# Attention scores with the low part of the keys as two 64-row products, and one score phase per head pair in the first layer

## The chip, the core and the metric

The kernel runs on one core of a Trainium2 chip. The metric is device microseconds (us) of one execution of the whole program; smaller is better. The time before is the median of three runs.

## The reference, cut to what matters

The program is a two-layer decoder trunk on 256 tokens of width 2048. Each layer normalises, projects to queries, keys, values and a gate, attends, multiplies by the gate, projects back and adds. The first layer ("fox") has 32 heads of 64 with a bias from cumulated forget gates; the second ("swa") has 32 query heads on 4 key heads, a window of 128 keys and a sink. The scores, which are the part that changes:

```python
# first layer, for each block of 128 queries
s = einsum('bqhd,bkhd->bhqk', qi, kf) * scale
s = s + ci[..., None] - c[:, :, None, :]
s = where(mask, s, NEG_INF); p = softmax(s)
# second layer
s = einsum('bqhgd,bnkhd->bnhgqk', qb, kw) * scale
s = where(mask, s, NEG_INF)
m = maximum(max(s), sink); e = exp(s - m)
p = e / (sum(e) + exp(sink - m))
```

## The kernel before, in words

**Two-part numbers.** Operands of the large products are split into a high part of reduced precision (type fp32r) and the low rest. Every weight tile `w`, 128 rows deep, comes from HBM as `wraw`; ScalarE copies the high part (line 224), VectorE subtracts to get the low part (line 225), and TensorE makes products of 512 columns (high by both parts) and of 256 columns (low by high) into PSUM tiles called `acc`. All matmuls are issued by one helper, line 83, so the profile shows them under that line and tells them apart by tile.

**Order of the work.** TensorE runs in program order. The projections stream without end; after every second matmul of a weight piece a step counter advances (`tick`), and work on attention is hung on it: `after(steps, fn)` runs `fn` that many steps later, with priority over the stream in the scheduler. The tables `FOX_DUE`, `FOX_LAST`, `FOX_ODD`, `FOX_FIRST`, `FOX_NEXT` (first layer, by group) and `SWA_DUE`, `SWA_LAST` (second) hold these step counts. A group is four heads: two pairs `j = 0, 1` of two heads `hh = 0, 1`. There are eight groups to a layer, so 16 pairs to a layer.

**Scores of a pair.** A head is 64 deep, half of the array's 128 rows. `stack_q` puts a head's high queries on one half of the rows and its low queries on the other half; the keys stand as `kk[hh]` with part 0 (high) and part 1 (low), each copied to both halves. One product on 128 rows thus gives (high + low) queries by one part of the keys. `product` takes both parts of the keys side by side, so its output has high and low keys in different columns, which VectorE adds.

In the first layer (`Pair`) a pair's scores come in two phases. `s` handles the second block of queries (128 queries, 256 keys): two products of 512 columns, a VectorE add of the low columns and the bias `bc` into the score tile `st` (line 432), and for each head a fused add of the high columns with a running maximum (line 413). `s_first` follows `second` steps later with the first block (128 queries, 128 keys): two products of 256 columns, an add (line 444), two fused adds. Then come the softmax, a 32x32 transpose on VectorE, and a trip through HBM by DMA to turn the probabilities (`pts`). In the second layer (`JointPair`) `s` handles both blocks in one phase: two products of 256 columns for the first block, and for the second block four products of 256 columns, high and low keys of each head added in PSUM.

**Buffers.** The scores of all pairs use one PSUM buffer of two banks (tag `S`, one bank a head); queries (`q2`) and keys (`kk`) of the first layer have one buffer each. The bias of a pair is fetched by a DMA on SP's queue and masked by GpSimd (line 127); `early` issues that, `bias` steps ahead of `s`.

**Narrow products.** The products of probabilities and values (`psy`, `psy_s`) use part of the array: 128 rows by 64 columns in the first layer, 32 by 64 in the second, each on its own part. The first layer also transposes a 32-row tile once (`pt_c`). The profile writes such a shape as rows*columns, 128*64 for instance; whole products show 128*128.

Of the kernel before, what the change touches and what calls it, by code (L numbers as in the profile page):

```python
# [10 lines left out]
F32 = mybir.dt.float32  # L11
# [5 lines left out]
P = 128  # L17
S = 256
# [3 lines left out]
HD = 64  # L22
# [11 lines left out]
FORGOT = 22  # L34

SINK = 8
BIAS = 14
SCALE_DUE = 8


FOX_DUE = ((22, 12, 20), (50, 13, 30), 150)
FOX_LAST = ((24, 12, 20), (48, 13, 30), 134)
FOX_ODD = ((27, 13, 25), (56, 13, 35), 118)
FOX_FIRST = ((57, 16, 32), (81, 12, 40), 185)
FOX_NEXT = ((32, 15, 25), (64, 14, 40), 120)
SWA_DUE = ((36, 65), (53, 81), 91)
SWA_LAST = ((36, 63), (51, 78), 86)

SECOND = 10
LAST_HALF = 8  # L50
HALVES = 2
QBUFS = 1
# [9 lines left out]
def trunk(  # L62
# [16 lines left out]
    nc = tc.nc  # L79


    def mm(*args, **kw):
        tc.keep_in_program_order(nc.tensor.matmul(*args, **kw))  # L83
# [9 lines left out]
    work = ctx.enter_context(tc.tile_pool(name="work", bufs=2))  # L93
    dram = ctx.enter_context(tc.tile_pool(name="dram", bufs=1, space=bass.MemoryType.DRAM))
    ps_acc = ctx.enter_context(tc.tile_pool(name="ps_acc", bufs=2, space=bass.MemoryType.PSUM))
    ps_s = ctx.enter_context(tc.tile_pool(name="ps_s", bufs=1, space=bass.MemoryType.PSUM))
# [12 lines left out]
    def after(steps, fn):  # L109
        due.setdefault(clock[0] + max(steps, 1), []).append(fn)  # L110
# [54 lines left out]
    class Unit:  # L165


        def __init__(self, pieces, kind, consume, n=256, acts=None, halves=True, stages=(), acc=None, apart=None):

            self.kind, self.consume, self.n, self.halves = kind, consume, n, halves
            self.stages, self.acc = stages, acc or (ps_acc, "acc")

            self.apart = apart
            self.acts = xs if acts is None else acts
            self.parts, kt = [], 0
            for src, sizes in pieces:
                off = 0
                for s in sizes:  # L180
                    self.parts.append((src, off, sum(sizes), kt, s))
                    off += s
                    kt += s
            assert kt == KT
            self.ps = [None, None]
# [28 lines left out]
    def load(unit, p):  # L214
        src, off, _, _, s = unit.parts[p]
        n = unit.n
        ask(unit, p, nc.sync)
        raw = unit.raw[:, off : off + s, :]
        w = wpool.tile([P, 2048], F32R, tag="w", name="w")
        w = w[:, 0 : 2 * s * n].rearrange("p (k h n) -> p k h n", h=2, n=n)  # L220
        high, low = w[:, :, 0, :], w[:, :, 1, :]
        if isinstance(src, tuple):
            high, low = (a.rearrange("p k (g n) -> p k g n", g=2) for a in (high, low))
        state["split"] = nc.scalar.copy(high, raw)  # L224
        state["lows"] = [*state.get("lows", [])[-1:], nc.vector.tensor_tensor(  # L225
            out=low, in0=raw, in1=high.bitcast(F32), op=ALU.subtract
        )]
        loaded[unit, p] = w
# [10 lines left out]
    def block(unit, p, c, wide_first=None):  # L239
# [19 lines left out]

        first, last = kt0 == 0, kt0 + s == KT  # L260
        ops = [operands(i) for i in range(s)]
        def done():
            if p < len(unit.parts) - 1:
# [91 lines left out]
    BLK = ((slice(0, P), 0), (slice(P, 3 * P), 1))  # L355
# [28 lines left out]
    TOP, BOTTOM = slice(0, HD), slice(HD, P)  # L384
# [9 lines left out]
    class Pair:  # L394
# [10 lines left out]
        def product(self, out, hh, qb, keys):  # L405

            q2, kk = self.operands()
            mm(out, q2[:, hh, qb * P : (qb + 1) * P], kk[hh][:, :, 0:keys], start=True, stop=True)

        def reduce(self, high, hh, rng, qb, low=None):  # L410

            st = self.st[:, hh, rng]
            nc.vector.tensor_tensor_reduce(  # L413
                out=st, in0=high, in1=st if low is None else low, scale=self.scale, scalar=self.start(hh),
                op0=ALU.add, op1=self.extreme, accum_out=self.mx[:, qb, hh : hh + 1],
            )
# [7 lines left out]
        def s(self):  # L424

            self.st = work.tile([P, 2, 3 * P], F32, tag="st", name="st")
            self.mx = work.tile([P, 2, 2], F32, tag="mx", name="mx")
            rng, qb = BLK[1]
            ps = ps_s.tile([P, 2, 512], F32, tag="S", name="ps_s")
            for hh in range(2):  # L430
                self.product(ps[:, hh], hh, qb, S)
            nc.vector.tensor_add(self.st[:, :, rng], ps[:, :, S:], self.bias[:, :, rng])
            for hh in range(2):
                self.reduce(ps[:, hh, 0:S], hh, rng, qb)
            after(self.second, self.s_first)

        def s_first(self):

            rng, qb = BLK[0]
            ps = ps_s.tile([P, 2, 512], F32, tag="S", name="ps_s")[:, 0, :]  # L440
            ps = ps.rearrange("p (h a k) -> p h a k", h=2, k=P)
            for hh in range(2):
                self.product(ps[:, hh], hh, qb, P)
            nc.vector.tensor_add(self.st[:, :, rng], ps[:, :, 1, :], self.bias[:, :, rng])
            for hh in range(2):
                self.reduce(ps[:, hh, 0, :], hh, rng, qb)
            self.soft(self.st, self.mx)
            self.turn()

        def turn(self):  # L450

            staged = fox.tile([P, NB, 6, B], F32, tag="staged", name="staged", bufs=1)
            nc.vector.transpose(
                staged.rearrange("p b t i -> p t b i"),
                self.st.rearrange("p h (t b i) -> p (h t) b i", b=NB, i=B),
            )
            turned_d = dram.tile([NB, P, 6 * B], F32, tag="turned_d", name="turned_d", bufs=2)
            nc.gpsimd.dma_start(
                out=turned_d.rearrange("b p x -> p b x"), in_=staged.rearrange("p b t i -> p b (t i)")
            )  # L460
            pts = self.group.new_pts(self.j)[:, self.j]
            for b in range(NB):
                nc.gpsimd.dma_start(  # L463
                    out=pts[b * B : (b + 1) * B], in_=turned_d[b].rearrange("(a j) x -> j a x", j=B)
                )

        def later(self, group, s, second=SECOND, bias=BIAS):
            self.group, self.second = group, second
            after(s - bias, self.early)
            after(s, self.s)  # L470

    class JointPair(Pair):
# [5 lines left out]

            return self.sinks[:, 1, hh : hh + 1]

        def s(self):
            self.st = work.tile([P, 2, 3 * P], F32, tag="st", name="st")
            self.mx = work.tile([P, 2, 2], F32, tag="mx", name="mx")
            ps = ps_s.tile([P, 2, 512], F32, tag="S", name="ps_s2")
            first = ps[:, :, S:].rearrange("p h (a k) -> p h a k", k=P)
            q2, kk = self.operands()
            for hh in range(2):
                self.product(first[:, hh], hh, 0, P)
            for hh in range(2):
                for part in range(2):  # L490
                    mm(
                        ps[:, hh, 0:S], q2[:, hh, P : 2 * P], kk[hh][:, part, :],
                        start=part == 0, stop=part == 1,
                    )
            (rng0, _), (rng1, _) = BLK
            nc.vector.tensor_add(self.st[:, :, rng0], first[:, :, 1, :], self.bias[:, :, rng0])
            for hh in range(2):
                self.reduce(first[:, hh, 0, :], hh, rng0, 0)
            for hh in range(2):
                self.reduce(ps[:, hh, 0:S], hh, rng1, 1, self.bias[:, hh, rng1])  # L500
            self.soft(self.st, self.mx)

        def later(self, group, s, t):
            after(s, self.s)
# [58 lines left out]
    ones_row, z, a = (once[0:H, i * S : (i + 1) * S] for i in range(3))  # L563
# [33 lines left out]
    class FoxGroup(Group):  # L597
# [14 lines left out]
        def k(self, ps):  # L612
# [12 lines left out]

            due = (FOX_FIRST, FOX_NEXT, FOX_DUE, FOX_ODD)[min(self.g, 2 + self.g % 2)] if self.g < 7 else FOX_LAST

# [70 lines left out]
    for g, G in enumerate(groups):  # L698
        if g == 0:
            half, gt, st = (work, "half", 2 * S, HALVES), (work, "gt", 2 * S, 3), (work, "st", 6 * P, 2)  # L700
# [377 lines left out]
    start = [(u, p) for p in range(4) for u in (v0, q0, k0)]  # L1078
# [153 lines left out]
```

## Time and profile before

| | |
|---|---|
| median of the runs | 803.98 us (803.02 to 804.32, three runs) |
| profiled execution, its own time | 802.76 us |
| its span, first to last instruction | 801.0 us |
| TensorE (PE) busy | 790.0 us, 99% of the span |
| VectorE (DVE) busy | 646.9 us, 81% |
| ScalarE (ACT) busy | 516.2 us, 64% |
| GpSimd (POOL) busy | 104.8 us, 13% |
| granted TensorE clock | 0.998 of full speed |

A row of the timeline gives the start in us, the length in us, the engine, the line, the operation, output and input tiles, shape, count, and idle time before it. PE is the matmul stream, PEld the weight loads that run beside it. Because matmuls are pipelined and a listed length covers the whole pipeline, lengths of neighbours overlap: the pace is read from one start to the next.

### The profile page before, as it was taken

The numbers are of one execution on the slowest core, as the hardware profiler recorded it, in microseconds if no ns is written. First come the engines' busy times: TensorE is split into PE (matmuls) and PEld (weight loads), VectorE is DVE, ScalarE is ACT, GpSimd is POOL, SyncE is SP. The second block draws the span as 40 slices with busy tenths as digits, with TensorE's granted clock in tenths as the row PEclk, the third lists the DMA queues.
The fourth block names the chain that finished last, engine by engine and source line by source line (L and its number), as shares of the span: only waits on it lengthen the run. The fifth ranks groups of instructions, "written<-read, shape, count | busy, mean of one in ns | idle before, by whom it ended". The sixth has DMA issues, their size and how long they took to land.

```text
span 801.0 us, 13775 instructions
## 1 busy us (share of the span) xinstructions
PE 790.0 (99%) x4994; PEld 695.3 (87%) x4994; DVE 646.9 (81%) x1150; ACT 516.2 (64%) x950; POOL 104.8 (13%) x166
## 2 busy tenths in 40 slices
PE   8999999999999999999999999999999999999995
PEld 7988888888888888888888888888888888888885
DVE  6988987888788877889739868668998999976654
ACT  7776656665657566567446656477788886875651
POOL 1001331021301112021203200200000000001210
PEclk9999999999999999999999999999999999999999
DMA  8757887596766968677756665855545554456632
GB/s 289 258 193 258 242 279 248 174 280 221 243 204 193 286 228 247 187 219 228 222 174 206 220 193 169 222 156 190 183 152 187 165 184 157 161 190 186 204 112 105
DMA packets 54052, 164.44 MB, mean 205 GB/s; under 512 B 7024, under 2 KB 10256, under 8 KB 53984
## 3 DMA queue, kind: packets, MB, share of 16 engines
q1 hardware_dynamic: 47376, 148.13, 57.6%
q0 software_dynamic: 5456, 13.97, 6.1%
q10 hardware_dynamic: 1152, 1.47, 0.5%
q8 instruction: 39, 0.64, 0.3%
q14 instruction: 29, 0.24, 0.1%
HBM read 154.84 MB, written 8.70 MB: 204 GB/s over the span
## 4 chain that ended last, share of the span: by engine, by line
PE 94%; DVE 2%; DMA 2%; ACT 1%; issue 0%; SPq 0%; DVEq 0%; ACTq 0%
PE acc L83 88%; PE ps_s L83 3%; PE psy L83 2%; DMA wraw<-in_fox_in_dram 1%; DMA wraw<-in_vf_dram 1%; DVE w L225 1%; PE psy_s L83 0%; ACT st L361 0%; ACT w L224 0%; DVE scaled L866 0%; DVE kk L623 0%; SPq L211 0%; ACT q L390 0%; DVE st L413 0%; DVE st L372 0%
## 5 line engine op out<-in xcount | busy, mean ns | idle before, releaser
L83 PE MATMUL acc<-xs,w 128*128 128x256 f32 (+1 forms) x2624 | 468.2, 337 | 0.0
L83 PEld LDWEIGHTS acc<-xs,w 128*128 128x128 f32 x2624 | 404.3, 190 | 52.9 <-issue 0.7
L225 DVE TENSOR_TENSOR w<-wraw,w 128x1024 fp32r<-128x1024 f32 (+4 forms) x280 | 323.0, 1170 | 85.4 <-ACT w L224 84.3
L224 ACT CAST w<-wraw 128x1024 fp32r<-128x1024 f32 (+4 forms) x280 | 274.7, 1000 | 168.8 <-PE acc L83 113.3
L83 PE MATMUL acc<-ys,w 128*128 128x256 f32 (+1 forms) x960 | 168.3, 337 | 0.0
L83 PEld LDWEIGHTS acc<-ys,w 128*128 128x128 f32 x960 | 147.7, 190 | 19.4 <-issue 0.5
L83 PE MATMUL acc<-w,xs 128*128 128x512 f32 (+2 forms) x512 | 107.6, 361 | 1.0 <-ACT w L224 1.0
L83 PEld LDWEIGHTS acc<-w,xs 128*128 128x128 f32 x512 | 87.1, 189 | 15.8 <-ACT w L224 1.7
L361 ACT ACTIVATE st<-st,mx 128x256 f32<-128x256 f32 (+1 forms) x128 | 56.6, 444 | 16.6 <-DVE mx L680 9.2
L319 ACT COPY half<-acc 128x512 f32<-128x512 f32 x56 | 32.6, 583 | 28.8 <-PE acc L83 28.1
L463 POOL DMA_DIRECT2D pts<-turned_d x64 | 35.0, 553 | 75.0 <-DMA turned_d<-staged 51.0
L127 POOL TENSOR_SCALAR_AFFINE_SELECT bc<-bc 128x256 f32<-128x256 f32 x32 | 20.0, 647 | 169.9 <-DMA bc<-negc_d 109.5
L771 POOL TENSOR_TENSOR acc<-acc,sq 128x256 f32<-128x256 f32 x28 | 26.6, 950 | 80.9 <-ACT sq L765 79.7
L769 POOL COPY acc<-sq 128x256 f32<-128x256 f32 x2 | 1.5, 754 | 243.1 <-ACT sq L765 243.1
L83 PE MATMUL ps_s<-kk,q 128*128 128x256 f32 (+1 forms) x160 | 30.6, 305 | 0.8 <-DVE kk L624 0.8
L83 PEld LDWEIGHTS ps_s<-kk,q 128*128 128x128 f32 x160 | 25.0, 190 | 3.9 <-ACT w L224 1.0
L361 ACT ACTIVATION_READ_ACCUMULATOR st<-st,mx 128x1 f32 x128 | 24.0, 188 | 0.0
L380 ACT ACTIVATE st<-st,rl 128x128 f32<-128x128 f32 x64 | 23.9, 446 | 0.1
L159 DVE SCALAR_TENSOR_TENSOR xs<-xT,g_sb,xs 128x256 fp32r<-128x256 f32 x32 | 20.7, 680 | 3.4 <-ACT xs L158 3.4
L413 DVE CUSTOM_DVE_ANT_0 st<-ps_s,st 128x256 f32<-128x256 f32 (+1 forms) x64 | 20.2, 350 | 0.5
L158 ACT ACTIVATE xs<-xT,g_sb 128x256 fp32r<-128x256 f32 x32 | 15.4, 500 | 7.0 <-DVE xT L740 6.3
L509 DVE STREAM_TRANSPOSE turned<-st 128x768 f32<-128x768 f32 x16 | 15.6, 975 | 4.2 <-ACT st L380 4.0
(142 smaller groups left out, 563.2 us busy)
## 6 DMA issues: line engine op xcount, KB each, us to landing
wraw<-in_fox_in_dram SPq DMA_DIRECT2D x96, 512.0 KB, 5.1
wraw<-in_swa_in_dram SPq DMA_DIRECT2D x72, 512.0 KB, 4.4
wraw<-in_swa_out_dram SPq DMA_DIRECT2D x32, 512.0 KB, 4.9
wraw<-in_fox_out_dram SPq DMA_DIRECT2D x29, 512.0 KB, 4.4
wraw<-in_fox_in_dram SPq DMA_DIRECT2D x54, 256.0 KB, 4.7
bc<-negc_d SPq DMA_DIRECT2D x16, 384.0 KB, 5.7
turned_d<-staged POOLq DMA_DIRECT2D x16, 384.0 KB, 5.0
pts<-turned_d POOLq DMA_DIRECT2D x64, 96.0 KB, 5.4
```

The lines of the kernel that those rows point to most:

```text
L83: tc.keep_in_program_order(nc.tensor.matmul(*args, **kw))
L127: return nc.gpsimd.affine_select(out=ap, in_=ap, compare_op=ALU.is_ge, fill=NEG, base=base, pattern=pattern, channel_multiplier=mult,)
L159: nc.vector.scalar_tensor_tensor(out=xs[:, kt, 1, :], in0=xT[:, kt, :], scalar=g, in1=xs[:, kt, 0, :].bitcast(F32), op0=ALU.mult, op1=ALU. ...
L224: state["split"] = nc.scalar.copy(high, raw)
L225: state["lows"] = [*state.get("lows", [])[-1:], nc.vector.tensor_tensor(out=low, in0=raw, in1=high.bitcast(F32), op=ALU.subtract)]
L319: nc.scalar.copy(s, ps[:, :, S : 2 * S])
L361: nc.scalar.activation(st[:, hh, rng], st[:, hh, rng], AF.Exp, scale=sign, bias=nm[:, qb, hh : hh + 1], accum_out=l[:, qb, hh : hh + 1],)
L380: nc.scalar.mul(st[:, hh, rng], st[:, hh, rng], rl[:, qb, hh : hh + 1])
L413: nc.vector.tensor_tensor_reduce(out=st, in0=high, in1=st if low is None else low, scale=self.scale, scalar=self.start(hh), op0=ALU.add, o ...
L463: nc.gpsimd.dma_start(out=pts[b * B : (b + 1) * B], in_=turned_d[b].rearrange("(a j) x -> j a x", j=B))
L509: nc.vector.transpose(turned.rearrange("p h k -> p (h k)"), self.st.rearrange("p h k -> p (h k)"))
L771: nc.gpsimd.tensor_add(sums[0], sums[0], s)
```

## The change

The low queries by low keys are no longer computed for the second block of queries. Each head's high queries (64 rows) are multiplied with its low keys by a product of 64 rows, `cross`; the one of head 0 stands on rows 0 to 63 of the array, the one of head 1 on rows 64 to 127, and they add into two different PSUM banks on top of the products with the high keys. Both layers now use one `s`: two products of 256 columns for the first block, two of 256 columns for the second block by high keys, and the two `cross` products. `s_first` is gone, and so is VectorE's 512-column add of the first layer; the bias of the second block enters through the fused add. The tables shift: a first-layer pair has its one phase 8 steps later than its first phase was, which is 4 to 8 steps before its second phase was.

```diff
-FOX_DUE = ((22, 12, 20), (50, 13, 30), 150)
-FOX_LAST = ((24, 12, 20), (48, 13, 30), 134)
-FOX_ODD = ((27, 13, 25), (56, 13, 35), 118)
-FOX_FIRST = ((57, 16, 32), (81, 12, 40), 185)
-FOX_NEXT = ((32, 15, 25), (64, 14, 40), 120)
+FOX_DUE = ((30, 20), (58, 30), 150)
+FOX_LAST = ((32, 20), (56, 30), 134)
+FOX_ODD = ((35, 25), (64, 35), 118)
+FOX_FIRST = ((65, 24), (89, 40), 185)
+FOX_NEXT = ((40, 25), (72, 40), 120)
...
+        def cross(self, out, hh, qb):
+            q2, kk = self.operands()
+            rows = (TOP, BOTTOM)[hh]
+            mm(
+                out, q2[rows, hh, qb * P : (qb + 1) * P], kk[hh][rows, 1, :], start=False, stop=True,
+                tile_position=(hh * HD, 0),
+            )
...
         def s(self):
             self.st = work.tile([P, 2, 3 * P], F32, tag="st", name="st")
             self.mx = work.tile([P, 2, 2], F32, tag="mx", name="mx")
-            rng, qb = BLK[1]
             ps = ps_s.tile([P, 2, 512], F32, tag="S", name="ps_s")
+            first = ps[:, :, S:].rearrange("p h (a k) -> p h a k", k=P)
+            q2, kk = self.operands()
             for hh in range(2):
-                self.product(ps[:, hh], hh, qb, S)
-            nc.vector.tensor_add(self.st[:, :, rng], ps[:, :, S:], self.bias[:, :, rng])
+                self.product(first[:, hh], hh, 0, P)
             for hh in range(2):
-                self.reduce(ps[:, hh, 0:S], hh, rng, qb)
-            after(self.second, self.s_first)
-
-        def s_first(self):
-            rng, qb = BLK[0]
-            ps = ps_s.tile([P, 2, 512], F32, tag="S", name="ps_s")[:, 0, :]
-            ps = ps.rearrange("p (h a k) -> p h a k", h=2, k=P)
+                mm(ps[:, hh, 0:S], q2[:, hh, P : 2 * P], kk[hh][:, 0, :], start=True, stop=False)
             for hh in range(2):
-                self.product(ps[:, hh], hh, qb, P)
-            nc.vector.tensor_add(self.st[:, :, rng], ps[:, :, 1, :], self.bias[:, :, rng])
+                self.cross(ps[:, hh, 0:S], hh, 1)
+            (rng0, _), (rng1, _) = BLK
+            nc.vector.tensor_add(self.st[:, :, rng0], first[:, :, 1, :], self.bias[:, :, rng0])
             for hh in range(2):
-                self.reduce(ps[:, hh, 0, :], hh, rng, qb)
+                self.reduce(first[:, hh, 0, :], hh, rng0, 0)
+            for hh in range(2):
+                self.reduce(ps[:, hh, 0:S], hh, rng1, 1, self.bias[:, hh, rng1])
             self.soft(self.st, self.mx)
             self.turn()
```

In `JointPair` the second layer's own `s` goes (it had the same shape, with four 128-row products for the second block), and `turn` does nothing there.

Three places show what moves. First TensorE's program order in the first layer's group 2 (`ps_s` are the scores, `q_1420` its stacked queries), before and then after:

```order
L83 MATMUL acc<-xs,w 128x256 x28
L83 MATMUL ps_s<-kk,q_1420 128x512 x2
L83 MATMUL acc<-xs,w 128x256 x4
L83 MATMUL acc<-xs,w 128x512 x20
L83 MATMUL ps_s<-kk,q_1420 128x256 x2
L83 MATMUL acc<-xs,w 128x512 x12
L83 MATMUL acc<-xs,w 128x256 x20
L83 MATMUL ps_s<-kk,q_1420 128x512 x2
L83 MATMUL acc<-xs,w 128x256 x12
L83 MATMUL acc<-xs,w 128x512 x14
L83 MATMUL ps_s<-kk,q_1420 128x256 x2
```

```order
L81 MATMUL acc<-xs,w 128x256 x32
L81 MATMUL acc<-xs,w 128x512 x12
L81 MATMUL ps_s<-kk,q_1420 128x256 x6
L81 MATMUL acc<-xs,w 128x512 x20
L81 MATMUL acc<-xs,w 128x256 x32
L81 MATMUL acc<-xs,w 128x512 x4
L81 MATMUL ps_s<-kk,q_1420 128x256 x6
```

Each pair's 2 + 2 products, with a stretch of the stream between them, became one run of six; the last two of the six are the 64-row ones.

Second, TensorE's order in the first layer's last group, 7 (stacked queries `q_3655`), where its first scores stand, before and then after:

```order
L83 MATMUL acc<-xs,w 128x512 x32
L83 MATMUL acc<-xs,w 128x256 x32
L83 MATMUL ps_s<-kk,q_3655 128x512 x2
L83 MATMUL acc<-xs,w 128x512 x16
L83 MATMUL acc<-w,xs 128x512 x8
```

```order
L81 MATMUL acc<-xs,w 128x512 x32
L81 MATMUL acc<-xs,w 128x256 x32
L81 MATMUL acc<-xs,w 128x512 x16
L81 MATMUL ps_s<-kk,q_3655 128x256 x6
L81 MATMUL acc<-w,xs 128x512 x16
```

Sixteen products of 512 columns now stand ahead of this group's first scores.

Third, VectorE's order for group 2's first pair, from the last low part ahead of the scores on, before and then after (`ISA` is the fused add with its maximum, and the row `mx` behind it the write of that maximum):

```order
L225 TENSOR_TENSOR w<-wraw,w 128x4x256 x2
L432 TENSOR_TENSOR st<-ps_s,bc 128x2x256
L413 ISA st,mx<-ps_s,st 128x256
L413 ISA mx 128x1
L413 ISA st,mx<-ps_s,st 128x256
L413 ISA mx 128x1
L225 TENSOR_TENSOR w<-wraw,w 128x4x256
L348 TENSOR_TENSOR gt<-acc,half 128x512
L444 TENSOR_TENSOR st<-ps_s,bc 128x2x128
L349 TENSOR_TENSOR gt<-gt,r_n_492 128x512
L413 ISA st,mx<-ps_s,st 128x128
```

```order
L223 TENSOR_TENSOR w<-wraw,w 128x4x256 x3
L445 TENSOR_TENSOR st<-ps_s,bc 128x2x128
L420 ISA st,mx<-ps_s,st 128x128
L420 ISA mx 128x1
L420 ISA st,mx<-ps_s,st 128x128
L420 ISA mx 128x1
L420 ISA st,mx<-ps_s,bc 128x256
L420 ISA mx 128x1
L420 ISA st,mx<-ps_s,bc 128x256
L420 ISA mx 128x1
L346 TENSOR_TENSOR gt<-acc,half 128x512
```

The 512-element add (128x2x256) is gone, and the reading of the scores is one block on VectorE instead of two with a low part between them.

More of the change, by code (lines that the diff above doesn't have):

```diff
@@ L36 @@
 SINK = 8
-BIAS = 14
 SCALE_DUE = 8
-FOX_DUE = ((22, 12, 20), (50, 13, 30), 150)
-FOX_LAST = ((24, 12, 20), (48, 13, 30), 134)
-FOX_ODD = ((27, 13, 25), (56, 13, 35), 118)
-FOX_FIRST = ((57, 16, 32), (81, 12, 40), 185)
-FOX_NEXT = ((32, 15, 25), (64, 14, 40), 120)
+FOX_DUE = ((30, 20), (58, 30), 150)
[3 more added lines that the diff above has]
+FOX_NEXT = ((40, 25), (72, 40), 120)
 SWA_DUE = ((36, 65), (53, 81), 91)
 SWA_LAST = ((36, 63), (51, 78), 86)
-SECOND = 10
 LAST_HALF = 8
@@ L465, in turn, with later @@
                 )
-        def later(self, group, s, second=SECOND, bias=BIAS):
-            self.group, self.second = group, second
+        def later(self, group, s, bias):
+            self.group = group
             after(s - bias, self.early)
@@ L479, in start, with turn @@
             return self.sinks[:, 1, hh : hh + 1]
[L481 to L501, printed above, removed]
+        def turn(self):
+            pass
         def later(self, group, s, t):
```

## Prediction

> **What bounds the kernel.** First the page's head, its busy times and the chain of work that ended last, then the list of who TensorE waited for:
>
> ```profile
> span 801.0 us, 13775 instructions
> PE 790.0 (99%) x4994; PEld 695.3 (87%) x4994; DVE 646.9 (81%) x1150; ACT 516.2 (64%) x950; POOL 104.8 (13%) x166
> PE 94%; DVE 2%; DMA 2%; ACT 1%; issue 0%; SPq 0%; DVEq 0%; ACTq 0%
> ...
> PE rows L83 <- DVE tail L852: 2.1, 1, 2.1
> PE warm L83 <- DVE ones L120: 1.1, 1, 1.1
> PE acc L83 <- ACT w L224: 1.0, 2, 0.6
> PE ps_s L83 <- DVE kk L624: 0.8, 1, 0.8
> ```
>
> TensorE is busy for 99% of the span, 94% of the chain is its own work, and of its waits those at the start (`warm`, `acc`) and the end (`rows`) lie outside what is changed. So each nanosecond that the matmul stream gains or loses between them is one of the total, and the only wait that the change touches is the last row. The other engines matter only if they begin to make TensorE wait.
>
> **What the scores cost on TensorE now.** The timeline, cut to PE, around a first-layer pair's two phases, then around a second-layer pair:
>
> ```profile
> 377.82 0.63 PE L83 MATMUL ps_s<-kk,q 128*128 128x512 f32 x2
> 378.29 1.58 PE L83 MATMUL acc<-w,xs 128*128 128x256 f32 x12
> ...
> 385.44 0.40 PE L83 MATMUL ps_s<-kk,q 128*128 128x256 f32 x2
> 385.68 1.55 PE L83 MATMUL acc<-w,xs 128*128 128x512 f32 x6
> ...
> 703.59 0.88 PE L83 MATMUL ps_s<-kk,q 128*128 128x256 f32 x6
> 704.31 2.92 PE L83 MATMUL acc<-ys,w 128*128 128x256 f32 x13
> ```
>
> From start to start: two products of 512 columns take 378.29 - 377.82 = 0.47 us, 0.235 each; two of 256 take 0.24; a first-layer pair 0.71. Six of 256 in the second layer take 0.72, 0.12 each. Weight loads don't show in this pace: each runs beside the product ahead of it.
>
> **The change on TensorE.** A pair becomes four whole products of 256 columns (0.48) and two of 64 rows. If the two run side by side they need one slot, 0.12, for both: 0.60 in all. That is the gain, 0.11 for a first-layer pair and 0.12 for a second-layer one. But a 64-row product doesn't use the array as the stream around it does, and the trace of before has places where TensorE goes from whole products to narrow ones and back. The nearest by shape is `pt_c`, 32 rows by 128 columns; the timeline of PE there, then of PEld:
>
> ```profile
> 51.66 0.40 PE L83 MATMUL acc<-xs,w 128*128 128x512 f32 x1
> 51.98 0.24 PE L86 MATMUL pt_c<-ident,c 32*128 32x32 f32 x1
> ...
> 52.22 0.39 PE L83 MATMUL acc<-xs,w 128*128 128x256 f32 x1
> ...
> 52.45 0.40 PE L83 MATMUL acc<-xs,w 128*128 128x256 f32 x2
> ...
> 51.43 0.19 PEld L83 LDWEIGHTS acc<-xs,w 128*128 128x128 f32 x1
> 51.98 0.20 PEld L86 LDWEIGHTS pt_c<-ident,c 32*128 32x128 f32 x2 [0.36 <-issue]
> ```
>
> From the last whole product of 512 columns (51.66) to the second whole product behind the visit (52.45) are 0.79 us. At the stream's pace this holds 0.235 + 0.12 and two products of 32 columns, some 0.03 each by the pace of `pt_r` below (an estimate): 0.41. So the visit costs 0.38 beside its own work. The PEld row shows why: the narrow weight load does not run beside the product ahead, it starts 0.36 us after the last load ended. The same on the way back: 52.22 to 52.45 is 0.23 for a product of 256 columns that otherwise takes 0.12, since its weights were loaded in the open. The second view is a visit of `psy`, 128 rows by 64 columns, first its way in, then its way out:
>
> ```profile
> 379.35 0.52 PE L83 MATMUL acc<-w,xs 128*128 128x256 f32 x3
> 379.79 0.44 PE L83 MATMUL psy<-pts,vg 128*64 128x256 f32 x2
> ...
> 380.06 0.39 PE L83 MATMUL psy<-pts,vg 128*64 128x256 f32 x2
> ...
> 382.39 0.27 PE L83 MATMUL psy<-pts,vg 128*64 128x128 f32 x1
> 382.60 0.39 PE L83 MATMUL acc<-w,xs 128*128 128x256 f32 x1
> ...
> 382.82 0.40 PE L83 MATMUL acc<-w,xs 128*128 128x256 f32 x2
> ...
> 492.44 0.60 PE L86 MATMUL pt_r<-ident,xT 128*128 128x128 f32 x4
> ...
> 492.77 0.27 PE L86 MATMUL pt_r<-ident,xT 128*128 128x128 f32 x1
> ```
>
> Way in: three whole products from 379.35 would end their slots at 379.71, the narrow one starts at 379.79, 0.08 late; its first step takes 0.27, while 256 columns of full precision take 0.22 by `pt_r` (three starts of 128 columns in 492.77 - 492.44 = 0.33, 0.11 each), so 0.05 late. Way out: 0.21 where 128 columns take 0.11, 0.10 late; then 0.22 where 0.12 is usual, 0.10 late. In all 0.33, with weights of 64 columns; `cross` loads 128 columns, as `pt_c` does. I take 0.38.
>
> Do the two halves run side by side? The whole `psy` visit:
>
> ```profile
> 379.79 2.87 PE L83 MATMUL psy<-pts,vg 128*64 128x256 f32 x32
> ```
>
> It covers sixteen steps of 256 and sixteen of 128 columns, 6144 columns, from 379.79 to 382.60: 2.19 columns a ns, against 128 / 0.11 = 1.16 for the whole products of the same precision. Two parts of the array do run at once here, 1.9 times the pace. I take the same for two row halves, which write two different banks.
>
> Each pair therefore goes to 0.60 + 0.38 = 0.98 us: first layer +0.27, second layer +0.26; 16 pairs each: 4.3 + 4.2 = **+8.5 us**. Bounds for this term: with no cost of the visit -0.11 x 16 - 0.12 x 16 = -3.7; with the visit at 0.33, +6.9; with the visit at 0.38 and the halves one after the other, 0.12 more for each of 32 pairs, +12.3.
>
> The Trainium skill ("TensorE: Matmul & The Clock Gate", section "Measured speedup vs the span model") gives products that are packed into tiles the time of one plus about 4 ns for each further tile, and has no term for going to tiles and back; by it this term would be the -3.7. The rows above disagree for so short a visit. The skill's page "TensorEngine Tiling (Array Packing)", section "Key Properties", says that a change of tiling mode drains the engine, without a figure; the 0.36 us of idle PEld is such a drain.
>
> **The wait that goes.** In group 7 the scores met keys that weren't ready:
>
> ```profile
> 366.90 0.39 PE L83 MATMUL ps_s<-kk,q 128*128 128x512 f32 x1
> 368.05 0.47 PE L83 MATMUL ps_s<-kk,q 128*128 128x512 f32 x1 [0.75 <-DVE kk L624]
> 368.35 2.92 PE L83 MATMUL acc<-xs,w 128*128 128x512 f32 x12
> ```
>
> From 366.90 to 368.35 are 1.45 us where the two products need 0.47. Now sixteen products of 512 columns stand ahead, 3.8 us, so the keys are there: **-1.0 us**. Nothing is late next at this place: the products moved ahead need only weights, and the weights are ready (below).
>
> **VectorE, ScalarE, queues.** The groups of VectorE by form, its wait for the casts, ScalarE's wait, and the bias transfer with its mask:
>
> ```profile
> L432 DVE TENSOR_TENSOR st<-ps_s,bc 128x512 f32<-128x512 f32 x16 | 10.9, 682 | 0.4 <-issue 0.2 <-PE ps_s L83 0.2
> ...
> L413 DVE CUSTOM_DVE_ANT_0 st<-ps_s,smask,sinks 128x256 f32<-128x256 f32 x32 | 14.2, 481 | 0.0
> ...
> L413 DVE CUSTOM_DVE_ANT_0 st<-ps_s,st 128x256 f32<-128x256 f32 x32 | 12.2, 415 | 0.3
> ...
> ACT w L224 <- PE acc L83: 113.3, 62, 4.0
> ...
> bc<-negc_d SPq DMA_DIRECT2D x16, 384.0 KB, 5.7
> ...
> L127 POOL TENSOR_SCALAR_AFFINE_SELECT bc<-bc 128x256 f32<-128x256 f32 x32 | 20.0, 647 | 169.9 <-DMA bc<-negc_d 109.5 <-DVE rl L369 29.8 <-DVE w L225 14.5
> ```
>
> VectorE loses 16 adds of 682 ns, 10.9 us. Its 32 wide fused adds now read the bias in place of `st`: between 415 ns (as now) and 481 (the second layer's, same shape), so 0 to +2.1 us; I take 415. All of it is off the path, since TensorE's list has no wait for VectorE but the one above: worth 0. The block of score reading grows by one part (0.42 + 0.57 of the first block added, 0.68 taken away, 0.3 us longer in one piece), and a low part behind it comes that much later. The cover is the stock of split weights: ScalarE waits 113.3 us in total for TensorE to give a weight buffer back, so weights are ahead of TensorE, not behind. Were that cover gone, it would be at most 0.3 x 16 = 5 us.
>
> The bias is asked for on SP's queue as many steps ahead of the scores as before (20 to 40), and passes the same weight loads with them; only group 0's first pair has 24 steps in place of 32. A step is two matmuls, (0.235 + 0.12) us on average, so 20 steps are 7.1 us against 5.7 + 0.65: it still fits. Softmax starts 4 to 8 steps sooner than now, so POOL's transfers of the turned probabilities start sooner, and `psy`, whose steps are unchanged, finds them ready as now: 0.
>
> **Sum.** +8.5 - 1.0 = +7.5 us. Against the profiled execution's own 802.76 us: 810.3. The median of the runs is 1.22 higher, 803.98, so **811.5 us**, 0.9% slower. A measurement of this kernel tells about 0.2%, 1.6 us, from no change.
>
> **Rivals.**
>
> No drain for row halves (faster): `cross` keeps all 128 columns and 64-row halves might join the stream with their weights loaded ahead. For it: the trace has no 64-row product, and the `pt_c` visit is a single one whose start could hide a wait. Against: its way back, 0.23, equals that of `psy`, where nothing was waited for. Place: the last two of each six. Price: -3.7 - 1.0 = -4.7, 799.3 us. It decides below a visit of 0.147 us ((3.7 + 1.0) / 32). By the skill's span rule this is the outcome.
>
> Halves one after the other: the `tile_position` halves don't overlap, because row halves share something that column halves don't. For it: no pair of row halves alone in the trace. Against: the `psy` pace. +12.3 - 1.0 = +11.3, 815.3 us.
>
> A half-priced visit: only the drains (0.08 + 0.10) are paid, and the weights of both ways are loaded under them. For it: the row halves have weights free to load on the other half. Against: 0.23 on both ways back. 0.18 gives first layer +0.07, second +0.06, 2.1 - 1.0 = +1.1: 805.1 us, inside 0.2%.
>
> **Chances.** Visit at the price of the rows, 0.75; one after the other, 0.09; half-priced, 0.06; no drain, 0.10. Slower: the first two and a little of the third, 0.85; same 0.05; faster 0.10. The likeliest reaches from +6.9 - 1.0 = 809.9 to about 813 with the weight stock slightly short; with the one-after-the-other case at 815.3 the range is 807 to 816.
>
> **What would show it.** Right: `ps_s` in a form of 64*128, 64 of them, a pair's two starts within 0.02 us; PEld idle some 0.2 to 0.4 us ahead of each; 0.22 us between the first two whole starts behind; 32 visits of near 0.98 us; line 432's group gone, the wait of `ps_s` for `kk` gone. Wrong: a pair of six in 0.61 us with weight loads unbroken; the halves 0.12 apart; or new waits of `acc` for `w`, or of `ps_s` for VectorE, which would mean that VectorE's longer block or the shifted steps cost more than the array's visits.

## The result, and the profile after

The changed kernel takes 812.33 us in the median of six runs against 804.03 us before; the ratio is 1.0097, with a 95% interval from 1.0083 to 1.0112. The forecast was 811.5, between 807 and 816. One of the six runs, the profiled one, had a TensorE clock of 0.66 and took 1126.1 us, so the ratio leaves it out and the rows below are those of the same kernel measured again at 0.997 (`after_again`). There it took 811.64 us against 804.34, ratio 1.0095 (1.0081 to 1.0109).

The head of its page, the chain, and the whole list of who TensorE waited for:

```profile
span 808.9 us, 13807 instructions
PE 798.7 (99%) x5026; PEld 696.6 (86%) x5026; DVE 637.8 (79%) x1134; ACT 516.2 (64%) x950; POOL 102.4 (13%) x166
PE 98%; DMA 1%; DVE 0%; SPq 0%; ACT 0%; DVEq 0%; issue 0%
...
PE rows L81 <- DVE tail L836: 2.1, 1, 2.1
PE warm L81 <- DVE ones L118: 1.1, 1, 1.1
PE acc L81 <- ACT w L222: 1.0, 2, 0.6
```

TensorE is still busy all the time, with 8.7 us more of it. VectorE has 9.1 us less, and the wait of `ps_s` for `kk` has left the list. No new wait of TensorE came: the kernel is slower although its busiest engine waits less. The length of the stream can be read without the start and the end of the kernel: from the first product of `pt_z`, which stands ahead of all scores, to the last product on `acc` it takes 748.4 us before (43.73 to 792.1) and 756.5 us after (43.50 to 800.0), 8.1 more. The groups that answer to the scores, by form:

```profile
L81 PE MATMUL ps_s<-kk,q 128*128 128x256 f32 x128 | 20.2, 280 | 0.0
L81 PE MATMUL ps_s<-kk,q 64*128 64x256 f32 x64 | 12.3, 379 | 0.0
L81 PEld LDWEIGHTS ps_s<-kk,q 64*128 64x128 f32 x64 | 6.0, 183 | 4.3
L420 DVE CUSTOM_DVE_ANT_0 st<-ps_s,bc 128x256 f32<-128x256 f32 x32 | 12.2, 419 | 0.0
```

The 64-row products stand there as 64*128, 64 of them, and the load of their weights has 4.3 us of idle time ahead of it, 0.13 for each of 32 pairs. The timeline of PE around one second-layer pair, whose like was shown at 703.59 before; the rows come from windows that begin a little later each time, so that single products show:

```profile
705.77 0.94 PE L81 MATMUL ps_s<-kk,q 128*128 128x256 f32 x6
...
706.12 0.59 PE L81 MATMUL ps_s<-kk,q 128*128 128x256 f32 x3
...
706.33 0.38 PE L81 MATMUL ps_s<-kk,q 64*128 64x256 f32 x2
706.64 0.50 PE L81 MATMUL acc<-ys,w 128*128 128x512 f32 x1
...
706.98 0.62 PE L81 MATMUL acc<-ys,w 128*128 128x512 f32 x2
```

The six products run from 705.77 to 706.64, 0.87 us. The last whole one starts at 706.12 and the 64-row pair at 706.33: 0.21 where the slot is 0.12. The pair, both in a row of 0.38 us that is no longer than one product, holds the stream until 706.64: 0.31 where one slot is 0.12. The first product behind starts there, and the next 0.34 later, where 512 columns take 0.23. Together 0.87 + 0.11 = 0.98 us, against 0.72 in the row of before.

### The profile page after: what moved, and what is told of

Its sections match the earlier page's. It is cut to its first block, busy times and chain, and to the rows that moved or that the text cites. A ratio compares the mean times of both kernels' runs of the same rounds, so it can differ in the third digit from the quotient of the medians.

```text
span 1123.1 us, 13807 instructions
## 1 busy us (share of the span) xinstructions
PE 1113.3 (99%) x5026; PEld 841.3 (75%) x5026; DVE 646.3 (58%) x1134; ACT 523.3 (47%) x950; POOL 104.2 (9%) x166
## 4 chain that ended last, share of the span: by engine, by line
PE 99%; DMA 0%; DVE 0%; ACT 0%; DVEq 0%; issue 0%; SPq 0%
PE acc L81 93%; PE ps_s L81 3%; PE psy L81 2%; PE psy_s L81 1%; DMA wraw<-in_vf_dram 0%; DVE scaled L850 0%; PE ps_n L81 0%; PE rows L81 0%; DVEq L1210 0%; PE pt_r L84 0%; PE ps_cols L81 0%; ACT w L222 0%; DVE tail_x L822 0%; DVE rest L826 0%; SPq L1030 0%
## 5 line engine op out<-in xcount | busy, mean ns | idle before, releaser
L81 PE MATMUL acc<-xs,w 128*128 128x256 f32 (+1 forms) x2624 | 654.6, 426 | 0.0
L81 PEld LDWEIGHTS acc<-xs,w 128*128 128x128 f32 x2624 | 488.6, 225 | 148.5 <-issue 44.8
L81 PE MATMUL acc<-ys,w 128*128 128x256 f32 (+1 forms) x960 | 236.4, 424 | 0.0
L81 PEld LDWEIGHTS acc<-ys,w 128*128 128x128 f32 x960 | 177.8, 225 | 57.1 <-issue 20.0
L81 PE MATMUL acc<-w,xs 128*128 128x512 f32 (+2 forms) x512 | 149.5, 462 | 0.6 <-ACT w L222 0.6
L81 PEld LDWEIGHTS acc<-w,xs 128*128 128x128 f32 x512 | 101.3, 214 | 43.0 <-issue 13.8
L81 PEld LDWEIGHTS ps_s<-kk,q 128*128 128x128 f32 (+1 forms) x192 | 30.4, 207 | 13.4 <-issue 7.8
L445 DVE TENSOR_TENSOR st<-ps_s,smask 128x256 f32<-128x256 f32 x16 | 6.8, 425 | 32.1 <-PE ps_s L81 32.1
L723 DVE TENSOR_TENSOR xT<-half,xT 128x512 f32<-128x512 f32 x15 | 11.4, 762 | 20.2 <-ACT half L317 20.2
L461 POOL DMA_DIRECT2D turned_d<-staged x16 | 12.4, 775 | 86.2 <-DVE staged L456 86.2
```

The source lines that it names most:

```text
L461: nc.gpsimd.dma_start(out=turned_d.rearrange("b p x -> p b x"), in_=staged.rearrange("p b t i -> p b (t i)"))
L723: nc.vector.tensor_add(x, low_half(ps), x)
```

## The experiments

**The changed kernel once more** (`after_again`, no edit).

> The changed kernel once more, for its trace at the full clock. Visits theory (each trip of TensorE from whole products to the 64-row pair and back costs 0.38 us beside its work, 32 of them): six products of a pair take 0.98 us or a little more, the two 64-row starts within 0.02 us, 8.3 us over before. Rival, serial halves (the 64-row products follow each other and the trip is cheaper): their starts 0.11 us apart. Rival, one phase (the joined score phase and the shifted steps cost, the tiles don't): the six take 0.61 us and new waits of TensorE for VectorE or for weights sum to some 12 us.

Measured: the rows above, 0.98 us for a pair; the other 31 pairs are within 0.01 us of it. Serial halves are out by the 706.33 row: two products in 0.38 us. The single phase as the culprit asked for new waits of some 12 us, and the wait list is shorter than before; the next run takes this rival out.

**The same with whole products** (`whole_cross`).

```diff
         def cross(self, out, hh, qb):
             q2, kk = self.operands()
-            rows = (TOP, BOTTOM)[hh]
-            mm(
-                out, q2[rows, hh, qb * P : (qb + 1) * P], kk[hh][rows, 1, :], start=False, stop=True,
-                tile_position=(hh * HD, 0),
-            )
+            mm(out, q2[:, hh, qb * P : (qb + 1) * P], kk[hh][:, 1, :], start=False, stop=True)
```

> As the changed kernel, but the two products of the low keys of the second block use all 128 rows again (both parts of the queries), so TensorE never leaves whole products for the scores; the single phase, VectorE's work and the steps stay as changed. Visits theory: six whole products, 0.72 us a pair, so +0.01 x 16 in the first layer, 0 in the second, and the 1.0 us wait of group 7 is gone: 0.8 us under before, some 803.2. Serial halves: the same here. One phase: stays at 812, as the phase and the steps are kept.

Measured 803.09 us, ratio 0.9986 (0.9976 to 0.9995), beside the 811.64 of the changed kernel. The phase, the steps and VectorE's work are those of the changed kernel; only the 64-row form is undone, and 8.5 us go with it. Its timeline at a second-layer pair:

```profile
697.92 0.88 PE L81 MATMUL ps_s<-kk,q 128*128 128x256 f32 x6
698.63 1.09 PE L81 MATMUL acc<-ys,w 128*128 128x512 f32 x4
```

Six whole products take 0.71 us. The product with twice the rows is the cheaper one here.

**Two trips a pair** (`two_visits`).

```diff
             for hh in range(2):
                 mm(ps[:, hh, 0:S], q2[:, hh, P : 2 * P], kk[hh][:, 0, :], start=True, stop=False)
-            for hh in range(2):
                 self.cross(ps[:, hh, 0:S], hh, 1)
```

> As the changed kernel, but each 64-row product stands right behind its own head's whole product: whole, whole, whole, narrow, whole, narrow. Two trips to narrow products a pair, with one narrow product each. Visits theory: the second trip adds 0.38 us and the second narrow product a slot of its own, 0.11 to 0.12: +0.5 us a pair, 16 us in all, some 828. Serial halves: the products were one after the other already, so only the cheap trip is added; at a trip of 0.26 (so that the measured 8.3 is met) 8.3 us, some 820. One phase: no change but lost overlap, under 4 us, some 816.

Measured 827.6 us, ratio 1.0292 (1.0278 to 1.0306). Same products, same inputs, another order:

```profile
720.89 1.45 PE L81 MATMUL ps_s<-kk,q 128*128 128x256 f32 x6
722.26 0.97 PE L81 MATMUL acc<-ys,w 128*128 128x512 f32 x3
```

1.37 us to the next product, 0.50 more than with one trip, 16 us for 32 pairs, and the times differ by 827.6 - 811.6 = 16.0 us. The price goes with the number of changes between whole and narrow products.

**One half left out** (`one_cross`).

```diff
             for hh in range(2):
-                mm(ps[:, hh, 0:S], q2[:, hh, P : 2 * P], kk[hh][:, 0, :], start=True, stop=False)
-            for hh in range(2):
-                self.cross(ps[:, hh, 0:S], hh, 1)
+                mm(ps[:, hh, 0:S], q2[:, hh, P : 2 * P], kk[hh][:, 0, :], start=True, stop=hh == 1)
+            self.cross(ps[:, 0, 0:S], 0, 1)
```

> As the changed kernel, but the second head's 64-row product of each pair is left out (that head's scores of the second block go without the low keys). Visits theory: it ran beside the first one, so leaving it out gives 0.01 us a pair, 0.4 us in all: 811.9. Serial halves: 0.11 to 0.12 us a pair, 3.6 us in all: 808.7. One phase: as visits, within 0.5 us of the changed kernel.

Measured 811.99 us, ratio 1.0095 (1.0079 to 1.011), the ratio that the changed kernel had beside it.

```profile
707.26 0.94 PE L81 MATMUL ps_s<-kk,q 128*128 128x256 f32 x5
708.13 1.19 PE L81 MATMUL acc<-ys,w 128*128 128x512 f32 x4
```

Five products take 0.87 us, as six did. The second half runs in the time of the first, so the packing works; it is the trip around it that costs.

**The pair twice in one trip** (`cross_twice`).

```diff
-        def cross(self, out, hh, qb):
+        def cross(self, out, hh, qb, last):
...
-                out, q2[rows, hh, qb * P : (qb + 1) * P], kk[hh][rows, 1, :], start=False, stop=True,
+                out, q2[rows, hh, qb * P : (qb + 1) * P], kk[hh][rows, 1, :], start=False, stop=last,
...
-            for hh in range(2):
-                self.cross(ps[:, hh, 0:S], hh, 1)
+            for last in (False, True):
+                for hh in range(2):
+                    self.cross(ps[:, hh, 0:S], hh, 1, last)
```

> As the changed kernel, but the pair of 64-row products is issued twice in the same trip (the low keys are added twice). Visits theory: the trip costs 0.38 us whatever is done in it, and a second pair of halves needs one more slot of 0.11 to 0.12 for both: +3.6 us over the changed kernel, some 815.3. Rival, the halves follow each other: two slots, +7.2 us, some 819. Rival, the price goes with each narrow product and not with the trip: the trip's 0.38 again, +12 us or more, some 824.

Measured 816.93 us, ratio 1.0152 (1.0136 to 1.0168). The median is 1.6 us above what was expected; by the ratios it is 4.6 us over the changed kernel, and the two intervals are too wide to tell that from 3.6. The timeline at a pair, and at the place of a new wait:

```profile
710.04 1.06 PE L81 MATMUL ps_s<-kk,q 128*128 128x256 f32 x8
711.03 0.96 PE L81 MATMUL acc<-ys,w 128*128 128x512 f32 x3
...
723.72 0.76 PE L81 MATMUL acc<-ys,w 128*128 128x256 f32 x5
725.20 0.98 PE L81 MATMUL acc<-ys,w 128*128 128x256 f32 x6 [0.72 <-DVE w L223]
```

The eight take 0.99 us: 0.12 more than the six for two more halves, 3.8 us for 32 pairs, as one slot each foretold. The rest is a new wait of TensorE for split weights behind the last scores, 0.72 us in the last row, which no other kernel here has: from `pt_z` to the last product on `acc` the stream takes 760.9 us, 4.4 more than the changed kernel's 756.5, and 3.8 and 0.7 make that up. Why the weights come late there stays open.

**Half of the weight columns** (`half_columns`).

```diff
             mm(
-                out, q2[rows, hh, qb * P : (qb + 1) * P], kk[hh][rows, 1, :], start=False, stop=True,
-                tile_position=(hh * HD, 0),
+                out[0:HD], q2[rows, hh, qb * P : qb * P + HD], kk[hh][rows, 1, :], start=False, stop=True,
+                tile_position=(hh * HD, 0), skip_group_check=True,
             )
...
-                mm(ps[:, hh, 0:S], q2[:, hh, P : 2 * P], kk[hh][:, 0, :], start=True, stop=False)
+                mm(ps[:, hh, 0:S], q2[:, hh, P : 2 * P], kk[hh][:, 0, :], start=True, stop=True)
```

> As the changed kernel, but the 64-row products load only 64 columns of weights (half of the queries get the low keys). Visits theory with its parts: about 0.10 us of the trip on the way in is the weight load in the open, and it goes with the columns: 0.05 us less a trip, 1.7 us in all, some 810. Rival, the price of the trip is drain alone and the weights load under it: the same time as the changed kernel, 811.6.

Measured 810.65 us, ratio 1.0072 (1.0056 to 1.0088). The times alone don't tell this from the changed kernel, as the intervals overlap; the timeline does:

```profile
705.14 0.89 PE L81 MATMUL ps_s<-kk,q 128*128 128x256 f32 x6
...
705.70 0.33 PE L81 MATMUL ps_s<-kk,q 64*64 64x256 f32 x2
705.96 1.42 PE L81 MATMUL acc<-ys,w 128*128 128x512 f32 x5
...
706.30 0.39 PE L81 MATMUL acc<-ys,w 128*128 128x512 f32 x1
```

From 705.70 to 705.96 are 0.26 us where 128 columns took 0.31, and the first step behind takes 0.34 as before. The stream from `pt_z` on takes 754.8 us, 1.7 less than the changed kernel's, as was expected. This fits a load of the narrow weights in the open, about 0.05 us for 64 columns. The form became 64*64 as well, so a shorter drain of the narrower form is not ruled out. The whole trip now costs 0.82 + 0.11 - 0.60 = 0.33 us, what the prediction read from `psy`, which also loads 64 columns.

**Before, with the last group's scores later** (`late_scores`, `later_scores`), beside the single phase with whole products once more (`whole_again`, same code as `whole_cross`). The first new line is that of 3 steps, the second that of 8:

```diff
-FOX_LAST = ((24, 12, 20), (48, 13, 30), 134)
+FOX_LAST = ((27, 12, 23), (48, 13, 30), 134)
...
+FOX_LAST = ((32, 12, 28), (56, 13, 38), 134)
```

> The kernel before with one number changed: the first scores of the first layer's last group come 3 steps later (24 to 27, the bias asked for at the same step as before). Both score phases, all whole products and VectorE's 512-column adds stay. If the 1.0 us wait for the keys is all that the single phase gained, this reaches what the single phase with whole products reached: 1.0 us under before, some 803.1 to 803.3. Rival: VectorE's relief (10.9 us less work) was worth something by itself, and then this stays above the single phase by that much, up to the whole 1.2 us: some 804.3.

> The kernel before, with the last group's two pairs 8 steps later, as in the changed kernel (24 to 32 and 48 to 56; the bias asked for at the same step). Three steps later had left 0.35 us of the wait for the keys. If that wait is all that a single phase with whole products gained, the six hundredths of a microsecond a pair apart (0.70 against 0.71 us of TensorE), this is as fast as that kernel or 0.2 us faster: 1.0 us under before. Rival: VectorE's relief is worth something beside it; then this stays behind the single phase by 0.4 us or more.

> The single phase with whole products once more, beside the kernel above on the same chip: 0.8 us under before if only the wait for the keys and TensorE's slots count, 1.2 us or more if VectorE's relief is worth something of its own.

Measured: 3 steps later 803.71 us, ratio 0.9987 (0.9973 to 1.0001), not clear of no change and above the 803.1 to 803.3 expected; 8 steps later **802.75 us**, ratio 0.9984 (0.9974 to 0.9993); beside that, whole products in one phase again 803.47, ratio 0.9993 (0.9982 to 1.0004). The "six hundredths" a pair of the second expectation are one, as its 0.70 and 0.71 say. The timeline where the wait was, 3 steps and then 8 steps later:

```profile
368.80 0.99 PE L83 MATMUL ps_s<-kk,q 128*128 128x512 f32 x2
369.62 0.63 PE L83 MATMUL acc<-xs,w 128*128 128x512 f32 x2
...
371.12 0.61 PE L83 MATMUL ps_s<-kk,q 128*128 128x512 f32 x2
371.57 3.79 PE L83 MATMUL acc<-w,xs 128*128 128x512 f32 x16
```

Three steps leave 0.82 us for two products that need 0.47; eight leave 0.45. The kernel before with one row of a table changed reaches what the single phase does, though VectorE keeps its 16 large adds: their 10.9 us were worth nothing that these runs can tell. The streams from `pt_z` on say the same: 748.4 us before, 747.9 with whole products in one phase, 747.6 with the scores 8 steps later. The kernel with the scores 8 steps later has the lowest median of all kernels here, under both the kernel before and the changed one; against `whole_again` the two intervals overlap.

## Why the prediction was right

**The term of the visit.** Put at 0.60 + 0.38 = 0.98 us a pair; measured 0.98. It was read from the one place where before went to 32 rows by 128 columns and back (`pt_c`), and the 64-row pair pays the same. That the middle of the visit came out alike has some luck in it: `pt_c` holds two products one behind the other (51.98 and 52.07), each with its own weights, and their work was an estimate. The parts that could be told apart: 0.09 late on the way in, some 0.10 of weight load in the open (an estimate, twice the 0.05 of `half_columns`), and on the way back 0.11 in the first step behind; what is left of the 0.38, some 0.08, is then the wait between the pair and the first whole load, which was not measured by itself. The Trainium skill's span rule ("TensorE: Matmul & The Clock Gate", section "Measured speedup vs the span model") counts about 4 ns for a further tile. Leaving a half out changed the run of products by less than the 0.01 us that the rows show, which agrees with the rule inside the trip; the trip is what it leaves out.

**Side by side.** Taken from column halves, where it was only a likeness; `one_cross` and `cross_twice` show it for row halves. The serial rival at 815.3 is out. So is the half-priced visit at 805.1: it put a visit at 0.18 us, and one costs 0.38.

**The wait that goes.** Put at -1.0 us; the wait is out of the list, and `later_scores` and the two runs of the single phase with whole products gained 1.3, 1.25 and 0.6 us. Sum: 31.4 us of scores against 22.9, less 1.0, is +7.5; the medians gave +8.3 and +7.3, the ratios +7.8 and +7.6, and the stream from `pt_z` on +8.1. By the stream the sum is 0.6 us short, and nothing larger than that was gained or lost elsewhere.

**VectorE at zero.** Right, by `later_scores`; the wide fused add with the bias takes 419 ns, where 415 was taken.

**What was off.** The idle time of PEld ahead of a pair was put at 0.2 to 0.4 us and is 0.13: the 0.36 of `pt_c` stood behind two products of 512 columns, each longer by 0.11, so that the load before had ended sooner and the last product went on longer; here two of 256 columns stand ahead. So the 0.36 us of idle PEld that the prediction called a drain were for the most part those products still running; the way in itself was 0.09 us late there (51.66 + 0.235 against 51.98), as it is here. The next step behind the trip is 0.34 instead of 0.22 us where 512 columns follow; the surplus, 0.11, is the same. The bias of a pair has two masks, 32 for 16 transfers, where the prediction's 5.7 + 0.65 us counted one; no wait of TensorE came of it. "The weights are ready" was too smooth for group 7, as shown below.

The rival without drain (799.3) failed on its condition: it needed a visit under 0.147 us, and a visit costs 0.38.

## What to carry to other kernels

The 64-row products in the midst of whole ones are priced by the trip, not by their columns: here a trip costs as much as three whole products of 256 columns, so saving one product by packing two halves loses. Pack only where many narrow products share one trip: the second pair of halves in the same trip cost 0.12 us where two whole products cost 0.24, so by these numbers it takes four packed pairs to earn the 0.38 of a trip (an estimate, not run). Price the trip ahead of time from the start-to-start times around the narrow product of the nearest form that the kernel already has. On an engine that is busy throughout, an overhead of this kind shows in no wait list, and the busy share stayed at 99%; the distance from one start to the next has it, and here the idle time of PEld ahead of the narrow loads points to it.

Not every product that leaves a part of the array unused pays. `pt_z` in the kernel before uses all rows and 32 columns:

```profile
43.61 0.28 PE L83 MATMUL acc<-xs,w 128*128 128x256 f32 x1
43.73 0.38 PE L86 MATMUL pt_z<-ident,vg 128*32 128x128 f32 x2
...
44.18 0.40 PE L83 MATMUL acc<-xs,w 128*128 128x512 f32 x1
```

The last row is the second whole product behind. From 43.61 to 44.18 are 0.57 us, and the slots in it, 0.12, twice 0.11 and 0.235, fill that. No run shows what spares it the price, so a product that only looks alike may mislead.

## What was not expected of the hardware

The reader was made later, and what it reads came later as well. With 3 steps, the scores came 1.9 us later (366.90 to 368.80), but the keys' last subtraction also came 1.3 us later (VectorE's timeline, before, then 3 steps later, then 8 steps later):

```profile
367.21 0.69 DVE L624 TENSOR_TENSOR kk<-k,kk 64x512 fp32r<-64x512 f32 x1
...
368.49 0.69 DVE L624 TENSOR_TENSOR kk<-k,kk 64x512 fp32r<-64x512 f32 x1
...
368.51 0.69 DVE L624 TENSOR_TENSOR kk<-k,kk 64x512 fp32r<-64x512 f32 x1
```

Of both delays 0.5 us belong to the whole stream, whose first scores already stand at 63.98 and 64.48 us; 1.4 and 0.8 are left. With 8 steps the keys come no later than with 3, and that is why 8 take the wait away. ScalarE shows where from, before and then 3 steps later:

```profile
358.37 1.05 ACT L224 CAST w<-wraw 128x1024 fp32r<-128x1024 f32 x1 [3.24 <-DMA wraw<-in_fox_in_dram]
...
361.37 0.58 ACT L319 COPY half<-acc 128x512 f32<-128x512 f32 x1
...
360.05 1.05 ACT L224 CAST w<-wraw 128x1024 fp32r<-128x1024 f32 x1 [4.34 <-DMA wraw<-in_fox_in_dram]
...
362.64 0.58 ACT L319 COPY half<-acc 128x512 f32<-128x512 f32 x1
```

The evacuation of the keys (line 319) stands right behind casts of weights whose transfer lands late, and the first of these casts starts 1.7 us later in the second kernel, 1.2 without the common 0.5. What TensorE waited for was thus a weight transfer, through two engines, and the list of waits names only the last of them. Why the transfer lands late there stays open; with one trace of each kernel it is not shown that the later scores are the reason.
